# A hybrid recurrent block on one core: RWKV-7 chunk maps combined ahead of the chain, buffers and PSUM banks reallotted

## The chip, the cores and the metric

One Trainium2 chip, one core. The metric is the device time of one execution in microseconds (us), the median of several runs.

## What is computed

Two layers over 1024 tokens of width 1024, batch 1, all in float32. Layer 0 mixes with a gated DeltaNet (GDN, 4 heads of 128) and an RWKV-7 group (8 heads of 64); layer 1 mixes with an RG-LRU. Each mixer and each SwiGLU FFN (width 2816) has adaptive norms around it. What the change touches is the RWKV-7 recurrence; per token and head, with a state `S` of 64 by 64:

```
def step(S, inp):
    r_t, w_t, k_t, v_t, kk_t, b_t = inp
    sa = -jnp.einsum('bhvk,bhk->bhv', S, kk_t)
    S = S * w_t[:, :, None, :] + sa[..., None] * b_t[:, :, None, :] + v_t[..., None] * k_t[:, :, None, :]
    return S, jnp.einsum('bhvk,bhk->bhv', S, r_t)
```

The kernel doesn't step by tokens but by chunks of 64: within a chunk the recurrence is a triangular system, whose inverse is made for all chunks at once, and a short chain then carries the state from chunk to chunk.

## The kernel before

The program is written with a framework that places instructions by their order in the program and by what is ready, gives each tile one of its tag's buffers, and sets all semaphores. Each engine then runs its own list in order, so an instruction that waits holds up what is behind it. A full-precision product is made of three float32r products (high by high, high by low, low by high); small products are plain float32, which the trace shows as two records each.

The two halves of the sequence (512 tokens, `h`) go through the mixer in 16 groups: for each half, four GDN heads and four pairs of RWKV heads, alternating. `mixer` (L947) runs three tasks per step beside each other: `inputs` of group n (projections in `mm` banks, 24 wide matmuls each), the first part of group n-1 (`gdn_first` L1219 or `rwkv_first` L1401, both around `inverse` L1164), and the second part of group n-2 (`gdn_second` L1288 or `rwkv_second` L1471, the chain). `together` (L151) hands out turns so that the tasks advance by their expected number of steps (`COUNTS`, L31). So a step with an RWKV chain has a GDN inverse beside it, and a step with an RWKV inverse has a GDN chain.

`rwkv_first` works on a pair of heads (head 0 on partitions 0 to 63, head 1 on 64 to 127) and all 8 chunks at once. `each` (L1410) issues sixteen 64 by 64 products into one bank of tag `sa` (three banks); `masked` and `turned` make masked score matrices and transposed operands. Its results are Z (the inverse), abq, btk, u, yv and kv. `rwkv_second` then does, for each chunk, three visits to TensorE with VectorE between them (banks of tag `sb`, two of them):

```
self.mm(pc[j, 0:64], ar[j, c, 0], S[j])
nc.vector.tensor_tensor(rhs, pc[:, 0:64], u[:, c], ALU.add)
self.mm(pc[j, 64:128], Z[j, c], rhs[j])
nc.vector.tensor_scalar(sa, pc[:, 64:128], -1.0, 0.0, ALU.mult, ALU.add)
self.mm(po[j, 0:64], btk[j, c], sa[j])
stt(S, po[:, 0:64], egc[:, c:c + 1], se, ALU.mult, ALU.add)
```

with two more products into `po` for the chunk's output, and norms and gate at the end of the eight chunks.

Other places that the change touches: `ffn.operands` (L696) makes the FFN's operand sums out of the second half of the tokens, with the transposes in `mm` banks (two of them) and all four work tiles of a round in tag `ad` (four buffers); `first` (L680) runs beside it and uses `mm` banks and two `e` buffers. `lru` (L808) makes, per block, two branch projections, four gate products and two z projections; all projections are in `mm` banks. `down` (L576) holds back the last `ntail` slices of its second half, so that each token tile finishes while matmuls of the next still run; at two places the held weights lie in tag `cy`.

Of the kernel before, what the change touches and what calls it, by code (L numbers as in the profile page):

```python
# [32 lines left out]
M_BANKS = ("mm", "mm", "es", "sa", "mm", "mm", "es", "sa")  # L33
G_TAGS = ("p",) * 6 + ("s1",) * 4 + ("cy",) * 6 + ("ar",) * 2 + ("s2",) * 2 + ("e",) * 2
RSCALE = 1024.0
# [37 lines left out]
class Block:  # L73
# [77 lines left out]
    def together(self, tasks):  # L151
# [12 lines left out]
        return out  # L164

    def gemm_fm(self, ps, w, xs):
        self.now(self.gemm_steps(ps, w, xs))
# [51 lines left out]
    def pair(self, tag):  # L219
        if tag == "ar":  # L220
# [420 lines left out]
    def ffn(self, l, hs):  # L641
# [54 lines left out]
        def operands(xs):  # L696

            tags = iter(("p",) * 12 + ("s1",) * 8 + ("cy",) * 12 + ("s2",) * 4)
            A = lambda: self.t("ad", [128, 512])
            for k in range(4):  # L700
                v12 = self.modulated(self.turned_x(xs, k), *self.AB, k, "ad")
                v22 = self.modulated(self.turned_x(xs, k + 4), *self.AB, k + 4, "ad")
                (h1, l1), (h2, l2) = b11[k], b21[k]
# [6 lines left out]
                for full, out in ((d2, t2), (d1, t1), (v12, t3), (v22, b22), (None, t4)):  # L710
                    if full is None:
                        tt(d2, f32(h2), d2, ALU.subtract)
                        tt(d2, d2, f32(l2), ALU.add)
                        full = d2
                    if out is t4 and k > 1:
                        hi, lo = self.pair("ar")
                    else:
                        hi, lo = self.t(next(tags), [128, 512], F32R), self.t(next(tags), [128, 512], F32R)
# [89 lines left out]
    def lru(self, h, hs):  # L808
# [16 lines left out]
        def branch(b):  # L825
            out = []
            for m in (2 * b, 2 * b + 1):
                ps = self.now(self.proj(w, 1024 + 128 * m, hs))
                cv = self.with_tail(ps, m, h)
                y = self.conv(ps, cv, lambda j: col["lru_conv_w"][:, 8 * j + m:8 * j + m + 1], col["lru_conv_b"][:, m:m + 1], "cy")  # L830
                out.append((y, self.split(y, "s1")))
            return out
# [3 lines left out]
        for b in range(4):  # L836
# [41 lines left out]
    def layers(self, hs, AB, x1, x2, x3, late):  # L878
# [4 lines left out]
        for n, (l, x_in, x_out) in enumerate(subs):  # L883
# [20 lines left out]
            for h in range(2):  # L904
# [24 lines left out]
                def aside():  # L929
# [3 lines left out]
                    elif n + 1 < len(subs):  # L933
# [13 lines left out]
    def mixer(self, x, x_out, mT, hs, AB):  # L947
# [7 lines left out]
        for W in (self.gW, self.rW):  # L955
            nc.gpsimd.memset(W, 0.0)
        self.pool_lo = 2
        groups = [(h, i) for h in range(2) for i in (0, 4, 1, 5, 2, 6, 3, 7)]
# [56 lines left out]
    def mix_out(self, h, x, x_out, mT, Gb, banks):  # L1015
# [12 lines left out]
        if h == 0:  # L1028
            self.down(lhs, self.a["mix_w_out"][0], h, x, x_out, Gb, banks)
        else:  # L1030
            return self.down(lhs, self.a["mix_w_out"][0], h, x, x_out, Gb, banks, "s2", ("cy", 6), True)

# [30 lines left out]

    def proj(self, w, c0, hs):
        ps = self.t("mm", [128, 512])
        yield from self.gemm_steps(ps, self.load_w(w, c0), hs)
        self.tick()
        return ps
# [274 lines left out]
    def rwkv_inputs(self, w, hs, sgd, wdad, p, h):  # L1343
# [26 lines left out]
        stt(rn, k, cl(self.col["rwkv_k_k"]), rn, ALU.mult, ALU.mult)  # L1370
        ar = self.t("ar", [128, 8, 2, 64])
        tt(ar[:, :, 0, :], c8(rn), eg[:, :, 0:64], ALU.mult)
        kf = E()
# [8 lines left out]
        r = self.shifted((yield from self.proj(w, 2056 + 128 * p, hs)), 12 + p, p, h, "e")  # L1382
        tt(ar[:, :, 1, :], c8(r), eg[:, :, 1:65], ALU.mult)
        stt(r, r, cl(self.col["rwkv_r_k"]), k, ALU.mult, ALU.mult)
# [16 lines left out]
    def rwkv_first(self, q):  # L1401
# [13 lines left out]
        def masked(x, tags):  # L1415
            lo, hi = self.t(tags[0], S8), self.t(tags[1], S8)
            for c0 in (0, 4):
                ps = bank()
                for c in range(4):
                    for j in hh:  # L1420
                        self.mm(ps[j, c * 128:c * 128 + 128], x[j, (c0 + c) * 64:(c0 + c) * 64 + 64], ar[j, c0 + c])
                yield
# [6 lines left out]
        def turned(x, tag):  # L1429
            ps = bank()  # L1430
            for i in range(4):
                self.tr(ps[:, i * 128:i * 128 + 128], x[:, i * 128:i * 128 + 128])
            yield
# [6 lines left out]

        ab, abq = yield from masked(bt, ("s1", "cy"))

# [4 lines left out]

        Z = yield from self.inverse(self.rlev, self.rtri, ab, bc(self.i64h), bc(self.i64), bc(self.i64s), prod, S8, self.rW, True)

        vtk = yield from turned(v, "s1")  # L1450
        ktk = yield from turned(kt, "s1")
        ak, akq = yield from masked(kt, ("s1", "s1"))
        pu = bank()
        each(pu, lambda j, c: ak[j, c], lambda j, c: vtk[j, c])
# [12 lines left out]
        nc.vector.tensor_tensor(kv, c8(pk), egc.unsqueeze(2).to_broadcast(S8), ALU.mult)  # L1467
        btk = yield from turned(bt, "cy")
        return Z, abq, btk, u, yv, kv

    def rwkv_second(self, q, carry, sgd, p, h):  # L1471
        nc = self.nc
        ar, bt, kt, v, bo, egc = q
        Z, abq, btk, u, yv, kv = carry
        stt = nc.vector.scalar_tensor_tensor
        hh = [slice(0, 64), slice(64, 128)]
        yT = self.t("s2", [128, 512])
        key = 4 + p
        if h == 0:
            S = self.t(f"S{key}", [128, 64])  # L1480
            nc.vector.memset(S, 0.0)
            self.S[key] = S
        for c in range(8):
            S = self.S[key]
            cs = slice(c * 64, c * 64 + 64)
            pc = self.t("sb", [128, 512])
            for j in hh:
                self.mm(pc[j, 0:64], ar[j, c, 0], S[j])
            yield
            se = self.t("ch", [128, 64])  # L1490
            stt(se, S, egc[:, c:c + 1], kv[:, c], ALU.mult, ALU.add)
            rhs = self.t("ch", [128, 64])
            nc.vector.tensor_tensor(rhs, pc[:, 0:64], u[:, c], ALU.add)
            for j in hh:
                self.mm(pc[j, 64:128], Z[j, c], rhs[j])
            yield
            sa = self.t("ch", [128, 64])
            nc.vector.tensor_scalar(sa, pc[:, 64:128], -1.0, 0.0, ALU.mult, ALU.add)
            po = self.t("sb", [128, 512])
            for j in hh:  # L1500
                self.mm(po[j, 0:64], btk[j, c], sa[j])
            for j in hh:
                self.mm(po[j, 64:128], S[j], ar[j, c, 1], stop=False)
            for j in hh:
                self.mm(po[j, 64:128], sa[j], abq[j, c], start=False)
            stt(S, po[:, 0:64], egc[:, c:c + 1], se, ALU.mult, ALU.add)
            self.act(yT[:, cs], po[:, 64:128], AF.Copy)
            yield
        nc.vector.tensor_tensor(yT, yT, yv.rearrange("p c n -> p (c n)"), ALU.add)
        pm = self.t("sb", [128, 512])  # L1510
# [41 lines left out]
```

## Time and profile before

| | us |
|---|---|
| median of 3 runs | 2840.73 |
| lowest, highest | 2827.24, 2842.32 |
| the profiled execution, its own time | 2827.93 |
| its span, first to last instruction | 2826.1 |
| TensorE busy | 2653.2 (94%) |
| VectorE busy | 1847.6 (65%) |
| ScalarE busy | 1258.8 (45%) |
| POOL busy | 659.3 (23%) |

Of the span, the mixer takes about the first 1000 us, the FFN of layer 0 and its sums run to about 1740, the RG-LRU stage to 2100, the second FFN to the end. In the profile PE is TensorE's matmuls, PEld its weight loads, DVE VectorE, ACT ScalarE, SP the queue that issues DMAs. Tile names have buffer numbers left out. The mean granted clock of TensorE was 0.977.

### The profile page before, as it was taken

Reading aid. Unit: us, or ns where it says so; the run is one execution under the profiler, and the core shown is the slowest. Engines: PE = TensorE matmul, PEld = TensorE weight load, DVE = VectorE, ACT = ScalarE, POOL = GpSimd, SP = SyncE. Lnnn points to the kernel's source line nnn. Section 1 sums busy time; section 2 is a strip of 40 time slices with the busy share of each in tenths; the row PEclk is TensorE's granted clock in tenths of the full one; section 3 lists DMA queues with packets and bytes.
Section 4 is the critical chain, followed back from the end, with each engine's and each line's share of the span. In section 5 each row is a group of like instructions: output and inputs, shape, how many; then the busy total and the mean of one; then the engine's idle time right before and its main releaser. Section 6 shows DMA issues by size and latency. Waiting matters only on the chain. (4 is left out here: it accounts for less than half of the span.)

```text
span 2826.1 us, 43754 instructions
## 1 busy us (share of the span) xinstructions
PE 2653.2 (94%) x16104; PEld 2049.9 (73%) x16104; DVE 1847.6 (65%) x3280; ACT 1258.8 (45%) x2300; POOL 659.3 (23%) x516
## 2 busy tenths in 40 slices
PE   6999999998999998899999999989898899999998
PEld 3666666666766766687888878777776788888887
DVE  5867778677687654998454463997874885444233
ACT  4555565553555535233332233664754333333222
POOL 2322221232322115333330000211214333331000
PEclk9999999999999999999999999999999999999999
DMA  7411222224521254666448873635334454448653
GB/s 234 120 44 56 61 79 61 68 57 135 161 57 53 69 186 138 225 214 209 145 138 294 293 253 117 198 105 167 102 111 149 147 194 151 141 134 290 230 188 109
DMA packets 402653, 415.75 MB, mean 147 GB/s; under 512 B 26331, under 2 KB 260606, under 8 KB 402438
## 3 DMA queue, kind: packets, MB, share of 16 engines
q1 hardware_dynamic: 402438, 412.95, 45.3%
q8 instruction: 127, 2.08, 0.3%
q14 instruction: 88, 0.72, 0.1%
HBM read 333.16 MB, written 79.69 MB: 146 GB/s over the span
## 5 line engine op out<-in xcount | busy, mean ns | idle before, releaser
L98 PE MATMUL mm<-ht,wh 128*128 128x512 f32 x2176 | 744.1, 417 | 52.7 <-ACT e L686 26.2
L98 PEld LDWEIGHTS mm<-ht,wh 128*128 128x128 f32 x2176 | 405.2, 194 | 156.0 <-ACT e L686 37.4
L98 PE MATMUL mm<-ht,wl 128*128 128x512 f32 x1088 | 446.6, 412 | 4.6 <-DVE wl L139 3.5
L139 POOL TENSOR_TENSOR wl<-wf,wh 128x512 fp32r<-128x512 f32 x144 | 207.9, 1446 | 552.6 <-ACT wh L138 417.3
L138 ACT CAST wh<-wd 128x512 fp32r<-128x512 f32 x206 | 127.3, 621 | 292.9 <-PE sb L98 219.4
L98 PEld LDWEIGHTS mm<-ht,wl 128*128 128x128 f32 x1088 | 210.8, 194 | 52.9 <-DVE wl L139 4.2
L660 POOL TENSOR_TENSOR wl<-wd,wh 128x512 fp32r<-128x512 f32 x99 | 132.6, 1339 | 487.4 <-ACT wh L659 447.8
L138 ACT CAST wh<-wf 128x512 fp32r<-128x512 f32 x215 | 133.3, 621 | 253.5 <-PE sb L98 83.2
L139 DVE TENSOR_TENSOR wl<-wd,wh 128x512 fp32r<-128x512 f32 x182 | 127.1, 700 | 167.8 <-ACT wh L138 167.7
L537 POOL TENSOR_TENSOR sm<-sm,dv 128x1 f32<-128x1 f32 x64 | 38.6, 611 | 510.9 <-DVE sm L535 277.0
L660 DVE TENSOR_TENSOR wl<-e,wh 128x512 fp32r<-128x512 f32 x88 | 62.7, 712 | 105.2 <-ACT wh L659 105.2
L98 PE MATMUL sa<-s,wh 128*128 128x512 f32 x392 | 122.9, 395 | 0.0
L659 ACT CAST wh<-wd 128x512 fp32r<-128x512 f32 x99 | 61.5, 622 | 124.2 <-PE sb L98 41.4
L106 ACT ACT_TABLE_LOAD x88 | 112.9, 1283 | 2.3 <-PEq L1541 0.7
L98 PEld LDWEIGHTS <-h 64*64 64x64 f16 (+1 forms) x1984 | 53.8, 106 | 80.5 <-issue 52.8
L659 ACT CAST wh<-yx 128x512 fp32r<-128x512 f32 x88 | 54.7, 622 | 126.8 <-PE sb L98 48.5
L106 ACT ACTIVATE e<-e 128x512 f32<-128x512 f32 x140 | 88.5, 632 | 47.4 <-DVE e L759 23.6
L106 ACT ACTIVATE e<-mm 128x512 f32<-128x512 f32 x120 | 71.4, 595 | 73.2 <-PE mm L98 70.5
L139 POOL TENSOR_TENSOR wl<-wd,wh 128x512 fp32r<-128x512 f32 x24 | 34.8, 1450 | 271.0 <-ACT wh L138 231.0
L139 DVE TENSOR_TENSOR wl<-wf,wh 128x512 fp32r<-128x512 f32 x71 | 48.9, 689 | 71.7 <-ACT wh L138 69.2
L98 PE MATMUL sa<-wh,p 128*128 128x512 f32 x260 | 91.5, 397 | 0.0
L767 ACT CAST yx<-yx 128x512 fp32r<-128x512 f32 x88 | 54.8, 623 | 77.4 <-DVE yx L764 42.1
(484 smaller groups left out, 6526.5 us busy)
## 6 DMA issues: line engine op xcount, KB each, us to landing
gd<-yx SPq DMA_DIRECT2D x176, 256.0 KB, 2.2
wd<-in_ffn_w_down_dram SPq DMA_DIRECT2D x132, 256.0 KB, 3.9
wf<-in_mix_w_in_dram SPq DMA_DIRECT2D x120, 256.0 KB, 2.8
wd<-in_ffn_w_gate_dram SPq DMA_DIRECT2D x114, 256.0 KB, 2.9
wd<-in_ffn_w_up_dram SPq DMA_DIRECT2D x78, 256.0 KB, 3.1
yx<-x SPq DMA_DIRECT2D x72, 256.0 KB, 4.2
ad<-in_ada_w_dram SPq DMA_DIRECT2D x63, 256.0 KB, 3.0
wf<-in_ffn_w_gate_dram SPq DMA_DIRECT2D x62, 256.0 KB, 3.1
```

Of the source, the lines that this page charges most:

```text
L98: self.nc.tensor.matmul(out, lhsT=lhsT, rhs=rhs, start=start, stop=stop, skip_group_check=more)
L106: return self.nc.scalar.activation(out, in_, func, bias=bias, scale=scale)
L138: nc.scalar.copy(wh, wf)
L139: (nc.gpsimd if self.pool_lo and (self.pool_lo > 1 or k0) else nc.vector).tensor_tensor(wl, wf, wh, ALU.subtract)
L537: nc.gpsimd.tensor_tensor(r, r, self.mhalf[:, 0:1], ALU.pow)
L659: nc.scalar.copy(flat(wh), full)
L660: (eng or nc.vector).tensor_tensor(flat(wl), full, flat(wh), ALU.subtract)
L767: nc.scalar.copy(hi, g)
```

## The change

For each chunk the state goes through one linear map. `rwkv_first` now builds, for all eight chunks: G = -(Z applied to the transposed a), P = identity + (G by btk) as a block-diagonal 128 by 128 matrix for the pair of heads, R = (G by abq) + r, nu = -(Z applied to u), and folds nu into yv and kv. A chain step is then one matmul of P with the state and one VectorE operation; the eight states are kept, and the outputs are sixteen products with R at the end. To make this, a fourth transposed operand is needed, and the two streams in `rwkv_first` (inverse, and the rest) advance beside each other. Tag PB is new (two buffers of twice the size, in which the two P lie during the mixer); s1 has six buffers in place of eight, cy ten in place of twelve, and later users of the tags follow.

```diff
-            self.tags(self.pool("work"), p=12, ar=2, s1=8, cy=12, s2=4, st=2, gb=2, ad=4)
+            self.tags(self.pool("work"), p=12, ar=2, PB=2, s1=6, cy=10, s2=4, st=2, gb=2, ad=4)
...
-            A = lambda: self.t("ad", [128, 512])
+            A = E
             for k in range(4):
-                v12 = self.modulated(self.turned_x(xs, k), *self.AB, k, "ad")
-                v22 = self.modulated(self.turned_x(xs, k + 4), *self.AB, k + 4, "ad")
+                v12 = self.modulated(self.turned_x(xs, k, ("sb", "es")), *self.AB, k, "ad")
+                v22 = self.modulated(self.turned_x(xs, k + 4, ("sa",)), *self.AB, k + 4, "ad")
...
-                ps = self.now(self.proj(w, 128 * m, hs))
+                ps = self.now(self.proj(w, 128 * m, hs, "sb"))
...
-                               "s2" if keep else "yx", ("cy", 6) if keep else ("ht", 7) if last else (None, 0), keep, aside)
+                               "s2" if keep else "yx", ("cy", 5) if keep else ("ht", 7) if last else (None, 0), keep, aside)
...
-        ar = self.t("ar", [128, 8, 2, 64])
+        ar = self.t("ar", [128, 2, 8, 64])
...
+        (Z, abq), (atk, vtk, akq, u, btk, ktk) = yield from self.beside(inverted(), others())
+        pg = bank()
+        each(pg, lambda j, c: Z[j, c], lambda j, c: atk[j, c])
         yield
-        u = self.t("cy", S8)
-        nc.scalar.copy(u, c8(pu))
+        G = self.t("yx", S8)
+        self.act(G, c8(pg), AF.Copy, scale=-1.0)
+        ph = bank()
+        each(ph, lambda j, c: Z[j, c], lambda j, c: u[j, c])
+        pr = bank()
+        each(pr, lambda j, c: G[j, c], lambda j, c: abq[j, c])
+        yield
+        nu = self.t("cy", S8)
+        self.act(nu, c8(ph), AF.Copy, scale=-1.0)
+        R = self.t("cy", S8)
+        nc.vector.tensor_tensor(R, c8(pr), ar[:, 1], ALU.add)
+        pp = bank()
+        each(pp, lambda j, c: G[j, c], lambda j, c: btk[j, c])
+        yield
+        P = self.rP[self.turn % 2]
+        self.turn += 1
+        for j in (0, 1):
+            nc.vector.tensor_tensor(P[hh[j], :, 64 * j:64 * j + 64], c8(pp)[hh[j]],
+                                    self.i64[hh[j]].unsqueeze(1).to_broadcast([64, 8, 64]), ALU.add)
+
+        def two(ps, f, g, f2, g2):
+            for c in range(8):
+                for j in hh:
+                    o = ps[j, c * 64:c * 64 + 64]
+                    self.mm(o, f[j, c], g[j, c], stop=False)
+                    self.mm(o, f2[j, c], g2[j, c], start=False)
+
         py = bank()
-        each(py, lambda j, c: vtk[j, c], lambda j, c: akq[j, c])
+        two(py, vtk, akq, nu, abq)
...
         pk = bank()
-        each(pk, lambda j, c: ktk[j, c], lambda j, c: vtk[j, c])
+        two(pk, ktk, vtk, btk, nu)
...
+        S = self.t("s2", [128, 8, 64])
+        nc.scalar.copy(S[:, 0], self.S[key])
+        pc = self.t("sb", [128, 512])
         for c in range(8):
-            S = self.S[key]
-            cs = slice(c * 64, c * 64 + 64)
-            pc = self.t("sb", [128, 512])
+            o = pc[:, c * 64:c * 64 + 64]
+            self.mm(o, P[:, c], S[:, c])
+            yield
+            stt(S[:, c + 1] if c < 7 else self.S[key], o, egc[:, c:c + 1], kv[:, c], ALU.mult, ALU.add)
+        po = self.t("sb", [128, 512])
+        for c in range(8):
             for j in hh:
...
+                self.mm(po[j, c * 64:c * 64 + 64], S[j, c], R[j, c])
+        yield
```

`beside` takes a step of each of two generators in turn. The moved instructions show in TensorE's list at two places.

The chain, in a step with a GDN inverse and RWKV projections beside it (`mm` is a projection, `sa` the inverse, `sb` the chain; moving operand first, weights second). Before:

```order
L98 MATMUL mm_2156<-ht_367,wh_2165 128x512
L98 MATMUL mm_2156<-ht_366,wl_2166 128x512
L98 MATMUL sb_2182<-ch_2197,cy_1699 64x64 x2
L98 MATMUL mm_2156<-ht_372,wh_2165 128x512
L98 MATMUL mm_2156<-ht_373,wh_2165 128x512
L98 MATMUL sb_2216<-ch_2214,cy_1885 64x64 x2
L98 MATMUL sb_2216<-ar_1074,S_370_1938 64x64 x2
L98 MATMUL sb_2216<-cy_1185,ch_2214 64x64 x2
L98 MATMUL mm_2156<-ht_372,wl_2166 128x512
```

and now (PB is P, s is the row of states, cy is R):

```order
L98 MATMUL sa_2153<-h_403_2125,W_432 128x64
L98 MATMUL sb_2202<-cy_1869,s_381_2061 64x64 x3
L98 MATMUL mm_2253<-ht_291,wh_2256 128x512
L98 MATMUL mm_2253<-ht_292,wh_2256 128x512
L98 MATMUL sb_2063<-s_381_2061,PB_436 128x64
L98 MATMUL sb_2202<-cy_1869,s_381_2061 64x64
L98 LDWEIGHTS h_402_2123
L98 MATMUL sa_2169<-h_404_2127,h_402_2123 128x64
```

The visits of two and of six narrow products are gone; a 128 by 64 product stands for them, and the output products are strewn between other work.

The end of the first part, in a step with a GDN chain beside it (`sa` with 64x64 is the RWKV pair of heads). Before:

```order
L98 MATMUL mm_2993<-ht_384,wh_3002 128x512
L98 MATMUL sa_3103<-s_577_3044,s_580_3065 64x64 x8
L98 MATMUL mm_2993<-ht_385,wh_3002 128x512
L98 MATMUL mm_2993<-ht_384,wl_3003 128x512
L98 MATMUL sa_3127<-s_581_3066,s_577_3044 64x64 x16
L98 MATMUL mm_3161<-ht_291,wh_3164 128x512
L98 MATMUL mm_3161<-ht_292,wh_3164 128x512
L98 MATMUL mm_3161<-ht_291,wl_3165 128x512
L98 MATMUL sa_3179<-s_577_3044,s_579_3060 64x64 x16
L98 MATMUL mm_3161<-ht_297,wh_3164 128x512
```

and now:

```order
L98 MATMUL sa_1822<-cy_1411,cy_1786 64x64 x15
L98 MATMUL sa_1839<-cy_1189,yx_1820 64x64 x16
L98 MATMUL sb_1858<-cy_1002,ch_1856 128x128
L98 MATMUL mm_1751<-ht_372,wh_1760 128x512
L98 MATMUL mm_1751<-ht_373,wh_1760 128x512
L98 MATMUL mm_1751<-ht_372,wl_1761 128x512
L98 MATMUL sa_1871<-cy_1458,yx_1820 64x64 x16
L98 MATMUL mm_1751<-ht_378,wh_1760 128x512
L98 MATMUL mm_1751<-ht_379,wh_1760 128x512
L98 MATMUL mm_1751<-ht_378,wl_1761 128x512
L98 MATMUL sa_1893<-s_278_1280,yx_1274 64x64
L98 MATMUL sa_1893<-cy_1189,cy_1867 64x64
```

Where blocks of sixteen stood, there are more of them, and the last two blocks alternate between two products that are summed in one place.

## Rows read from the trace of the kernel before

**Rows 1.** the page, busy time by engine, share of the span, instructions
```profile
PE 2653.2 (94%) x16104; PEld 2049.9 (73%) x16104; DVE 1847.6 (65%) x3280; ACT 1258.8 (45%) x2300; POOL 659.3 (23%) x516
```

**Rows 2.** the chain that ended last, one piece: start, us, engine, tile, line, matmuls
```profile
2216.60 2.72 PE sa L98 x12
```

**Rows 3.** windows, RWKV-chain step, GDN-chain step: busy PE, PEld, DVE, ACT, POOL; clock, DMA
```profile
192.00:248.00 56.00, 52.03 (x425) 35.36 (x424) 42.05 (x92) 29.94 (x59) 15.18 (x11) 0.97 0.16 43
248.00:292.00 44.00, 43.46 (x571) 32.01 (x570) 34.43 (x68) 28.41 (x53) 11.52 (x9) 1.00 0.27 80
```

**Rows 4.** TensorE in order of time in an RWKV-chain step: start, us, tiles, records
```profile
974.49 0.39 PE L98 MATMUL mm<-ht,wl 128*128 128x512 f32 x1
974.81 0.33 PE L98 MATMUL sb<-ch,cy 64*64 64x64 f32 x4
974.98 0.28 PE L98 MATMUL sb<-ar,S 64*64 64x64 f32 x4
975.09 0.28 PE L98 MATMUL sb<-cy,ch 64*64 64x64 f32 x4
975.30 0.73 PE L98 MATMUL mm<-ht,wh 128*128 128x512 f32 x2
975.88 0.39 PE L98 MATMUL mm<-ht,wl 128*128 128x512 f32 x1
...
976.46 0.73 PE L98 MATMUL mm<-ht,wh 128*128 128x512 f32 x2
977.12 0.33 PE L98 MATMUL sb<-ch,cy 64*64 64x64 f32 x4
977.38 0.50 PE L98 MATMUL mm<-ht,wl 128*128 128x512 f32 x1
```

**Rows 5.** the same in a GDN-chain step: narrow blocks, transposes, GDN chain
```profile
964.96 3.06 PE L98 MATMUL sa<-s,s 64*64 64x64 f32 x96 [0.44 <-ACT s L1438]
967.96 0.66 PE L101 MATMUL sa<-k,p 128*128 128x128 f32 x4
968.45 0.39 PE L98 MATMUL sb<-ch,cy 128*128 128x128 f32 x2
968.67 0.39 PE L98 MATMUL sb<-cy,S 128*128 128x128 f32 x2
968.89 0.39 PE L98 MATMUL sb<-cy,ch 128*128 128x128 f32 x2
969.04 0.48 PE L98 MATMUL mm<-ht,wh 128*128 128x512 f32 x1
```

**Rows 6.** tile ch on VectorE: duration ns min/median/max, first and last start
```profile
L1491 DVE SCALAR_TENSOR_TENSOR ch<-S,egc,cy x64: 269/279/1309, 187.9 to 996.5; 128x64 f32<-128x64 f32 x64
L1493 DVE TENSOR_TENSOR ch<-sb,cy x64: 209/218/226, 195.7 to 997.3; 128x64 f32<-128x64 f32 x64
L1498 DVE TENSOR_SCALAR ch<-sb x64: 206/225/227, 197.8 to 999.3; 128x64 f32<-128x64 f32 x64
```

**Rows 7.** waits of TensorE in the mixer, 110 to 1003 us: total, times, longest
```profile
PE sa L98 <- DVE h L1192: 10.9, 9, 1.6
PE sb L98 <- DVE ch L1493: 7.0, 7, 1.6
```

**Rows 8.** RG-LRU stage: a wait of TensorE, and windows of both halves
```profile
PE mm L98 <- DVE cy L857: 9.6, 3, 5.5
...
1760.00:1910.00 150.00, 137.73 (x605) 111.67 (x604) 138.55 (x265) 99.91 (x164) 28.38 (x24) 0.97 0.46 147
1940.00:2090.00 150.00, 136.15 (x572) 109.00 (x572) 135.15 (x219) 94.14 (x155) 27.27 (x23) 0.94 0.44 140
```

**Rows 9.** FFN operands: waits of TensorE in both layers, window of the first
```profile
PE mm L98 <- ACT e L686: 9.4, 5, 4.6
...
PE mm L98 <- ACT e L686: 8.7, 4, 4.6
...
1100.00:1150.00 50.00, 34.68 (x126) 26.23 (x125) 39.24 (x44) 23.15 (x41) 26.02 (x17) 0.83 0.38 121
```

More of the change, by code (lines that the diff above doesn't have):

```diff
@@ L33 @@
 M_BANKS = ("mm", "mm", "es", "sa", "mm", "mm", "es", "sa")
[L34 removed]
+G_TAGS = ("p",) * 6 + ("s1",) * 3 + ("cy",) * 5 + ("PB",) * 2 + ("ar",) * 2 + ("s2",) * 2 + ("e",) * 2
 RSCALE = 1024.0
@@ L164, in together, with beside @@
         return out
+    def beside(self, a, b):
+        left, out = {0: a, 1: b}, {}
+        while left:
+            for j, steps in list(left.items()):
+                try:
+                    next(steps)
+                except StopIteration as e:
+                    out[j] = e.value
+                    del left[j]
+            yield
+        return out[0], out[1]
     def gemm_fm(self, ps, w, xs):
@@ L219, in pair @@
     def pair(self, tag):
-        if tag == "ar":
+        if tag in ("ar", "PB"):
             u = self.t(tag, [128, 2, 512], F32R)
@@ L714, in operands @@
                         full = d2
-                    if out is t4 and k > 1:
-                        hi, lo = self.pair("ar")
+                    if out is t4:
+                        hi, lo = self.pair("ar" if k > 1 else "PB")
                     else:
@@ L830, in branch @@
                 y = self.conv(ps, cv, lambda j: col["lru_conv_w"][:, 8 * j + m:8 * j + m + 1], col["lru_conv_b"][:, m:m + 1], "cy")
-                out.append((y, self.split(y, "s1")))
+                out.append((y, self.split(y, "PB" if m % 2 else "s1")))
             return out
@@ L956, in mixer @@
             nc.gpsimd.memset(W, 0.0)
+        self.turn = 0
+        self.rP = [self.t("PB", [128, 8, 128]) for _ in range(2)]
+        for P in self.rP:
+            nc.gpsimd.memset(P, 0.0)
         self.pool_lo = 2
@@ L1030, in mix_out @@
         else:
-            return self.down(lhs, self.a["mix_w_out"][0], h, x, x_out, Gb, banks, "s2", ("cy", 6), True)
+            return self.down(lhs, self.a["mix_w_out"][0], h, x, x_out, Gb, banks, "s2", ("cy", 5), True)
     def mixer_params(self, w):
@@ L1062, in with_tail, with proj @@
         return cv
-    def proj(self, w, c0, hs):
-        ps = self.t("mm", [128, 512])
+    def proj(self, w, c0, hs, bank="mm"):
+        ps = self.t(bank, [128, 512])
         yield from self.gemm_steps(ps, self.load_w(w, c0), hs)
@@ L1431, in turned @@
             for i in range(4):
-                self.tr(ps[:, i * 128:i * 128 + 128], x[:, i * 128:i * 128 + 128])
+                self.tr(ps[:, i * 128:i * 128 + 128], x(i))
             yield
@@ L1439, in turned @@
             return y
-        ab, abq = yield from masked(bt, ("s1", "cy"))
+        pair = lambda x: lambda i: x[:, i * 128:i * 128 + 128]
         def prod(ps, x, y):
@@ L1446, in prod, with inverted @@
                     self.mm(ps[j, c], x[j, c], y[j, c])
[L1448 to L1454, printed above, removed]
-        yield
-        u = self.t("cy", S8)
-        nc.scalar.copy(u, c8(pu))
+        def inverted():
+            ab, abq = yield from masked(bt, ("s1", "cy"))
+            Z = yield from self.inverse(self.rlev, self.rtri, ab, bc(self.i64h), bc(self.i64), bc(self.i64s), prod, S8, self.rW, True)
+            return Z, abq
@@ new lines, in others @@
+        def others():
+            atk = yield from turned(pair(ar[:, 0].rearrange("p c n -> p (c n)")), "yx")
+            vtk = yield from turned(pair(v), "yx")
+            ak, akq = yield from masked(kt, ("s1", "s1"))
+            pu = bank()
+            each(pu, lambda j, c: ak[j, c], lambda j, c: vtk[j, c])
+            yield
+            u = self.t("cy", S8)
+            nc.scalar.copy(u, c8(pu))
+            btk = yield from turned(pair(bt), "cy")
+            ktk = yield from turned(pair(kt), "yx")
+            return atk, vtk, akq, u, btk, ktk
@@ L1467, in rwkv_first @@
         nc.vector.tensor_tensor(kv, c8(pk), egc.unsqueeze(2).to_broadcast(S8), ALU.mult)
-        btk = yield from turned(bt, "cy")
-        return Z, abq, btk, u, yv, kv
+        return P, R, yv, kv
     def rwkv_second(self, q, carry, sgd, p, h):
@@ L1473, in rwkv_second @@
         ar, bt, kt, v, bo, egc = q
-        Z, abq, btk, u, yv, kv = carry
+        P, R, yv, kv = carry
         stt = nc.vector.scalar_tensor_tensor
         hh = [slice(0, 64), slice(64, 128)]
-        yT = self.t("s2", [128, 512])
         key = 4 + p
         if h == 0:
-            S = self.t(f"S{key}", [128, 64])
-            nc.vector.memset(S, 0.0)
-            self.S[key] = S
-        for c in range(8):
-            S = self.S[key]
-            cs = slice(c * 64, c * 64 + 64)
-            pc = self.t("sb", [128, 512])
-            for j in hh:
[L1488 to L1508, printed above, removed]
@@ L1509, in rwkv_second @@
-        nc.vector.tensor_tensor(yT, yT, yv.rearrange("p c n -> p (c n)"), ALU.add)
+            self.S[key] = self.t(f"S{key}", [128, 64])
+            nc.vector.memset(self.S[key], 0.0)
+        S = self.t("s2", [128, 8, 64])
+        nc.scalar.copy(S[:, 0], self.S[key])
+        pc = self.t("sb", [128, 512])
+        for c in range(8):
+            o = pc[:, c * 64:c * 64 + 64]
+            self.mm(o, P[:, c], S[:, c])
+            yield
+            stt(S[:, c + 1] if c < 7 else self.S[key], o, egc[:, c:c + 1], kv[:, c], ALU.mult, ALU.add)
@@ L1510, in rwkv_second @@
+        po = self.t("sb", [128, 512])
+        for c in range(8):
+            for j in hh:
+                self.mm(po[j, c * 64:c * 64 + 64], S[j, c], R[j, c])
+        yield
+        yT = self.t("s2", [128, 512])
+        nc.vector.tensor_tensor(yT, po, yv.rearrange("p c n -> p (c n)"), ALU.add)
         pm = self.t("sb", [128, 512])
```

8 lines of the change are left out of this document (4 added, 4 removed).

## The prediction

> **What bounds the kernel now.** I read the page first, then busy time in windows, then the waits, then the instructions of TensorE in order of time. The page gives TensorE 94% of the span [rows 1]. That figure is flattering, since ends of matmuls are modelled and a matmul whose successor stands waiting still counts. A better measure is the spacing of starts: in the chain that ended last, twelve matmuls of 512 columns take 2.72 us, 0.227 us each [rows 2], and wherever starts follow at that step TensorE is the bound.
>
> The windows show that the mixer alternates between two kinds of steps [rows 3]. In the first kind (call it A) the program puts the RWKV chain of one head pair beside the GDN inverse of the next heads and the RWKV projections of the ones after. In the second kind (B) it puts the GDN chain beside the RWKV inverse and the GDN projections. A takes 56 us, with 425 matmul records, B takes 44 us with 571. There are eight of each. A has fewer matmuls and is longer: its TensorE stands in small waits and in changes between wide and narrow matmuls. B is packed; what is added there is paid in full. This decides the case, because the change takes matmuls out of A and puts more into B.
>
> **What leaves A.** A chunk of the chain had three visits of 64-row matmuls on TensorE. The visit with twelve records stands between wide matmuls: from 974.49 to 975.88 us there are three wide ones (0.68) in 1.39 us, so the visit costs 0.71 [rows 4]. The visit of four records: from 976.46 to 977.38 us there are two wide ones (0.45) in 0.92, so 0.47 [rows 4]. Twelve records back to back would be about 0.39 (0.17, 0.11, 0.11 between their starts), so some 0.3 us of a visit is going in and out. A chunk is 0.71 + 2 x 0.47 = 1.65 us; times 8 chunks and 8 head pairs, 106 us. To this come TensorE's waits for the sum before the second visit, 7 us [rows 7]. Together 113 us.
>
> **What takes its place in A.** One matmul per chunk, 128 rows by 128 columns, with 64 moving columns: two records. The trace has no such shape; the nearest is the GDN chain's two records of 128 by 128, which start 0.22 us apart from the next pair and pass into wide matmuls with no 0.3 us in between [rows 5]. I take 0.25 us: 64 x 0.25 = 16 us (0.22 to 0.52 each: 14 to 33). The sixteen output matmuls of a head pair stay narrow, and the order above shows them strewn in ones, twos and threes, about ten visits. Ten visits with half of them beside other narrow matmuls cost about 8 x 0.3 + 16 x 0.06 = 3.2 us, 26 us in all; in one block they would cost 1.3 (10 us), each alone 5.8 (46 us). So 42 us stand where 113 stood: **minus 71 us** (minus 34 to minus 89).
>
> **What B gets.** Ninety-six narrow records (three blocks of sixteen matmuls) take 3.00 us back to back, 1.0 us a block [rows 5]; in and out adds the 0.3 of above. Four new blocks (the products G, h, R and P): 5.2 us. The two blocks that become sums of two products double: each gets sixteen more matmuls, and now two matmuls of the same head follow each other. Four records of two heads take 0.17 us, which are three slots of 0.055 [rows 4]: only the records at a change of head overlap. A chunk of four matmuls then has six slots, 0.34 us, and the block 2.7 in place of 1.0: 3.4 us for both. Four more transposes take 0.5 [rows 5]. That is 9.1 us a head pair, and over eight **plus 73 us** (52 if all runs dense and overlapped, 88 if the sums don't overlap at all).
>
> So TensorE's own account of the mixer is even: plus 2 us, between minus 37 and plus 54. What tips it is small. VectorE loses three of four chain operations, 0.28, 0.22 and 0.22 us [rows 6], 46 us in all, and gets about 2 us a head pair for R and P. A has VectorE at 42 of 56 us [rows 3], and the waits of TensorE for it that are not the chain's are led by the inverse's masked copies, 10.9 us [rows 7]. I take minus 8 (0 to minus 15). A's granted clock is 0.97 and B's 1.00 [rows 3]; of the 1.7 us that this costs each A, I take back 5 us in all (0 to 10). ScalarE swaps eight small copies for four transposed copies, two full ones and a small one; it is busy 30 of 56 us [rows 3], and costs nothing unless it falls behind in B. The two memsets on POOL lie before the first chain, where POOL is a quarter busy; zero. The mixer: **minus 11 us**.
>
> **Outside the mixer.** In the RG-LRU stage the z projections move from the two mm banks to the two sb banks. TensorE waited 9.6 us for VectorE to give back an mm bank there [rows 8]; its order doesn't change. But VectorE is busy 139 and 135 of 150 us in the two halves [rows 8], so a wait that goes leaves at most 11 and 15 us until VectorE itself is the pace, and I take minus 8 (0 to minus 15). When the FFN operands are made, TensorE waited 9.4 and 8.7 us for ScalarE's copy out of an mm bank, which stood behind casts, which stood behind the four ad buffers [rows 9]. The change gives the transposes other banks and the differences the eight e buffers, two rounds ahead in place of one. VectorE has 39 of 50 us there [rows 9]; I take minus 7 and minus 6 (together plus 4 to minus 25). What is late next is VectorE in both. The held tail of two down projections loses one of six slices, 12 wide matmuls of cover or 2.7 us [rows 2] in each; it covers work that is short, so plus 2 (0 to 5). Loads of gated values only change tiles: zero, DMA is a matter of the same bytes.
>
> **Sum.** Minus 11, 8 and 13, plus 2: minus 30 us. The profiled execution took 2827.9 us (2826.1 of span); the median of the three runs is 2840.7, 12.8 above. So 2798 by the one and **2811 us** by the other, which is what I forecast, 1.1% faster. A measurement here can tell about 0.5%, 14 us: faster means under 2826.5, slower over 2855.
>
> **Rivals.** *Slower: three sa banks for two streams.* In B the inverse holds two sa banks at a time, and now seven other products and transposes run beside it on the same three. TensorE takes instructions in order, so a bank not yet copied out stops the projections too. Such waits exist: nine on the inverse, 1.2 us each [rows 7]. One for each of seven new users in eight head pairs is 67 us: 2878 us. It decides from three such waits a head pair on, since 3 x 8 x 1.2 eats the 30 us. Against it: ScalarE and VectorE have a third of B free [rows 3]. Chance 0.13. *A doesn't shrink.* TensorE is relieved there, but the weights, the inverse's chain and VectorE keep A near its length, and only 25 us of the 71 come back: 2811 + 46 = 2857. For it: A's other waits; against: VectorE has a quarter of A free. Chance 0.07. *No change.* The mixer is even and the waits outside only move to VectorE, minus 5 in all instead of minus 21, and the mixer's small gains fail: 2838. Chance 0.17. *B hides the added work.* Weight loading is busy 32 of B's 44 us [rows 3]; if the 12 us left were room, the 73 us would cost nothing: 2738. Starts at the full step speak against it; chance 0.05. The Trainium skill (Perfetto Trace Analysis, Identifying the Most-Contended Engine) would judge TensorE's headroom this way, by the busy share of weight loads and not of matmuls.
>
> My forecast has the remaining 0.58. Its own spread is about 20 us either way, so some 0.07 of it lies above 2826.5. Faster: 0.51 + 0.05 + 0.05 of the third rival = 0.61. Same: 0.07 + 0.12 + 0.02 = 0.21. Slower: the rest of the first two, 0.18. The range is 2765 to 2855: below lie the last rival and a little more, above the first and half of the second.
>
> **What would show it.** Right: A near 47 us and B near 53; new narrow blocks of 32 records near 1.0 to 1.3 us and of 64 near 2.7; chain matmuls 0.22 to 0.3 before the next start; no wait of TensorE for the z operation in the RG-LRU stage and VectorE near full there. Wrong: A still over 52 us, or B over 58 with waits on sa banks, or blocks of 64 records near 2 or near 4 us.

## The result: 1.2% slower, and the profile after

The changed kernel takes 2866.82 us (median; 2862.11 to 2875.37), the kernel before, measured beside it, 2838.07. The ratio is 1.0116, 95% interval 1.0092 to 1.0141. The forecast was 2811 us, the range 2765 to 2855: the time moved the other way, and out of the range. The profiled execution of the changed kernel took 2868.7 us (span 2866.9); before it was 2827.9, which is 10 us under that kernel's median, so the two profiles lie 41 us apart and the medians 29.

Where the 41 us between the two profiled executions lie, by the last finishing sum of a half's residual (L604 before, L617 now), the first gate sum of an FFN (L744, L757) and the RG-LRU's first and last product (L874, L887), each by its start:

| stretch | before | after | difference |
|---|---|---|---|
| start to the end of the mixer's output map | 1064.1 | 1110.3 | +46.2 |
| from there to the FFN's first gate sum (operands, layer 0) | 84.6 | 77.1 | -7.5 |
| from there to the first RG-LRU product | 658.1 | 663.4 | +5.3 |
| first to last RG-LRU product | 271.5 | 266.7 | -4.8 |
| from there to the last finishing sum | 53.9 | 56.8 | +2.9 |
| operands, layer 1 | 81.9 | 81.0 | -0.9 |
| the rest | 612.0 | 611.6 | -0.4 |

One profile of each kernel gives the mixer's loss only roughly. Two of the experiments below leave the mixer as it was: up to 1000 us, TensorE's list in e4 is that of the kernel before, and in e3 that of the changed kernel. Their output maps end at 1075.8 and 1101.0 us, so the loss is some 25 to 46 us. The 5.3 us in the third row are not the change's: in e8 and e13, which have the old code there, this stretch takes 663.7 and 664.0 us.

The page's first part, answering to [rows 1]: 672 matmul records more, and VectorE's total a little down.

```profile
PE 2673.6 (93%) x16776; PEld 2102.3 (73%) x16776; DVE 1838.6 (64%) x3112; ACT 1252.4 (44%) x2283; POOL 663.1 (23%) x518
```

The loss is in the mixer. Windows of the changed kernel, an A step, a B step and the next A (columns as in [rows 3]):

```profile
203.00:252.00 49.00, 44.09 (x225) 30.45 (x223) 31.28 (x57) 23.46 (x40) 11.93 (x9) 0.81 0.17 44
252.00:312.00 60.00, 57.92 (x858) 46.59 (x856) 42.21 (x82) 32.45 (x67) 11.78 (x9) 0.98 0.21 59
312.00:360.00 48.00, 42.57 (x227) 29.39 (x227) 33.54 (x57) 25.09 (x44) 13.12 (x10) 0.86 0.24 66
```

A is about as long as forecast (47), but with 225 records. By the prediction's own account it should have had 425 - 160 + 48 = 313; some 90 records of it now run in B, which is 60 us and not 53. So where A and B meet has moved, and the pair tells more: 109 us where 100 stood before, and where 100 were forecast. A has half the records of before and seven eighths of the time. And its granted clock has fallen from 0.97 to 0.81 and 0.86.

What happens in A is plain in TensorE's list where the chain begins (start, us, tiles, records; in brackets the idle time before, and who ended it):

```profile
324.27 0.62 PE L98 MATMUL mm<-ht,wh 128*128 128x512 f32 x2
324.73 0.39 PE L98 MATMUL mm<-ht,wl 128*128 128x512 f32 x1
327.60 0.43 PE L98 MATMUL sb<-s,PB 128*128 128x64 f32 x2 [2.49 <-ACT s L1537]
327.85 0.48 PE L98 MATMUL mm<-ht,wh 128*128 128x512 f32 x1
...
330.14 0.69 PE L98 MATMUL sb<-cy,s 64*64 64x64 f32 x6
330.76 1.22 PE L98 MATMUL mm<-ht,wh 128*128 128x512 f32 x2
331.77 0.52 PE L98 MATMUL sb<-s,PB 128*128 128x64 f32 x2
332.23 0.47 PE L98 MATMUL sb<-cy,s 64*64 64x64 f32 x2
332.63 0.40 PE L98 MATMUL sa<-h,h 128*128 128x64 f16 x4
332.96 0.47 PE L98 MATMUL sb<-cy,s 64*64 64x64 f32 x2
333.36 0.79 PE L98 MATMUL mm<-ht,wl 128*128 128x512 f32 x1
```

The first chain product waits 2.49 us. What follows is narrow, with few wide matmuls between, and from 329.3 us the granted clock is at 1.2 GHz for 13.7 us: two wide matmuls from 330.76 to 331.77 take 0.5 us each, where 0.23 is the full step. In the 15 us between the first chain product and the last there are 14 wide matmuls, 3.2 us of work at that step. In all eight chains together there are 117 wide matmuls in 104 us, some 15 a chain.

But the clock fell in five of the eight only: these take 13 to 18 us, at a granted clock of 0.52 to 0.65, and before four of them TensorE waits 2.2 to 2.5 us. The other three (at 553.5, 837.1 and 1026.7 us) wait 0.1 to 1.0 us, stay at 1.00 and take 8 to 10 us. Nor does the order alone settle it. The fifth chain has the same list and the same wait of 2.50 us in the changed kernel and in e3; here is the stretch behind that wait in the one and in the other:

```profile
674.00:690.00 16.00, 16.00 (x92) 11.87 (x92) 5.97 (x18) 3.66 (x8) 1.27 (x1) 0.50 0.10 34
...
669.00:680.00 11.00, 10.74 (x95) 7.98 (x95) 6.36 (x19) 4.31 (x11) 1.29 (x1) 1.00 0.14 51
```

Why the first chain product waits: ScalarE's copy of the carried state (L1537) stands in ScalarE's list behind an activation that waits for VectorE's scan of the projections (L1377):

```profile
323.04 0.69 ACT L106 ACTIVATE e<-es,dv 128x512 f32<-128x512 f32 x1 [0.47 <-PE es L98]
326.72 0.63 ACT L106 ACTIVATE e<-e 128x512 f32<-128x512 f32 x1 [3.00 <-DVE e L1377]
327.31 0.24 ACT L1537 COPY s<-S 128x64 f32<-128x64 f32 x1
```

TensorE's waits from 110 to 1000 us, longest first (engine, tile, line, waited for: total us, times, longest). Those on the chain's VectorE sum [rows 7] are gone; the copy leads in their place:

```profile
PE sb L98 <- ACT s L1537: 11.2, 6, 2.5
PE sa L98 <- DVE h L1216: 8.5, 7, 2.6
```

What the lower level costs can be read where TensorE, after a long idle time, runs wide matmuls alone (changed kernel, end of the mixer): starts 0.43 us apart, then 0.24.

```profile
1048.61 0.80 PE L98 MATMUL mm<-wh,p 128*128 128x512 f32 x1 [5.53 <-DVE p L110]
...
1051.69 0.63 PE L98 MATMUL es<-wh,p 128*128 128x512 f32 x1
1052.11 0.63 PE L98 MATMUL es<-wl,p 128*128 128x512 f32 x1
1052.54 0.60 PE L98 MATMUL es<-wh,p 128*128 128x512 f32 x1
1052.97 0.41 PE L98 MATMUL sb<-wh,p 128*128 128x512 f32 x1
1053.21 0.40 PE L98 MATMUL sb<-wl,p 128*128 128x512 f32 x1
```

From 110 to 1050 us the clock was at 1.2 GHz for 41 us before and for 97 us after; at nearly half speed the 56 us more are worth up to 28. In the second profile of each mixer (e4, e3) it was 55 and 92 us, so a difference of some 15 us between two kernels in this figure can be chance.

The diff does not show what set this order: `COUNTS` (L31) is not in it. `together` gives the next turn to the task with the smallest share of its expected steps done. The line says 25 steps for the chain and 28 for the RWKV first part. The changed code has 9 and 21; before it had 24 and 23. So the chain gets its nine turns in the first 36% of A, and the first part is through after three quarters of B.

### The profile page after: what moved, and what is told of

The parts are those of the page before. It is cut to its first block, busy times and chain, and to the rows that moved or that the text cites. A ratio compares the mean times of both kernels' runs of the same rounds, so it can differ in the third digit from the quotient of the medians.

```text
span 2866.9 us, 44925 instructions
## 1 busy us (share of the span) xinstructions
PE 2673.6 (93%) x16776; PEld 2102.3 (73%) x16776; DVE 1838.6 (64%) x3112; ACT 1252.4 (44%) x2283; POOL 663.1 (23%) x518
## 5 line engine op out<-in xcount | busy, mean ns | idle before, releaser
L98 PE MATMUL mm<-ht,wh 128*128 128x512 f32 x1920 | 664.7, 422 | 31.1 <-ACT e L699 20.3
L98 PEld LDWEIGHTS mm<-ht,wh 128*128 128x128 f32 x1920 | 359.5, 196 | 121.4 <-ACT e L699 32.3
L98 PE MATMUL mm<-ht,wl 128*128 128x512 f32 x960 | 394.1, 413 | 11.3 <-DVE wl L139 10.1
L98 PEld LDWEIGHTS mm<-ht,wl 128*128 128x128 f32 x960 | 187.3, 195 | 53.7 <-DVE wl L139 11.8
L98 PEld LDWEIGHTS <-h 64*64 64x64 f16 (+1 forms) x1984 | 60.4, 108 | 92.6 <-issue 51.3
L98 PE MATMUL sb<-p,wh 128*128 128x512 f32 x264 | 82.7, 395 | 5.8 <-DVE yx L759 5.8
```

The lines of the kernel that those rows point to most:

```text
L98: self.nc.tensor.matmul(out, lhsT=lhsT, rhs=rhs, start=start, stop=stop, skip_group_check=more)
```

## The experiments

The theories. **T1**: the chain's order in A (stall, few wide matmuls around narrow ones, lower clock) is the loss. **T2**: the added narrow work in B is the loss, and A is bound by other things. **T3**: the edits outside the mixer. Medians are set beside the kernel before as run in the same batch.

**e1_direct_state.** The copy stays, but the first chain product no longer needs it:

```diff
-            self.mm(o, P[:, c], S[:, c])
+            self.mm(o, P[:, c], S[:, c] if c else self.S[key])
```

> The first chain matmul of a head pair reads the carried state itself; ScalarE's copy of it stays, but only the output products need it. In the changed kernel TensorE stands 2.5 us there in five of the first six RWKV-chain steps looked at or less, and works at half the granted clock right behind. Theory 1 (the stall and the clock that falls behind it are the loss): the waits for that copy go, 8 x 2.5 = 20 us at least, and the time at half clock (211 us) falls by 30 to 50 us, worth half of that: 2825 to 2850 us. Theory 2 (the added narrow work in the other steps is the loss, and the chain's steps are bound by the inverse and VectorE): the idle moves to the next wait, 2860 to 2870. Theory 3 (the edits outside the mixer): no change, 2867.

2841.14 us, ratio to before 1.0024 (0.9996 to 1.0051): 26 us under the changed kernel. It is not the wait itself that came back: listed waits of TensorE between 110 and 1000 us sum to 65 us, against 67. The first wait of the chain shrank, others (L1209, 10.3 us) grew:

```profile
PE sb L98 <- ACT s L1537: 3.4, 3, 1.5
```

But the first chain product now stands earlier in the list (201.7 us, in place of 218.5), some 37 wide matmuls lie between the first product and the last in place of 15 (most of them before the second; the other seven products keep 9 to 15 among them), and the time at 1.2 GHz over the whole run falls from 210 to 152 us. Of these 58 us, 55 lie before the end of the mixer's output map, which comes 26 us earlier. 58 us of it gave 26, 0.45 each, with waits and output visits (65, against 71) nearly unchanged. The Trainium skill (TensorE: Matmul & The Clock Gate, HAM oscillation — how this bites in real kernels) counts half of the time at the lower clock as lost; that would be 29 us here, as an estimate, and this run agrees within what it can tell.

**e2_counts.** The one line the change had left alone:

```diff
-COUNTS = ((33, 24, 13), (25, 28, 25))
+COUNTS = ((33, 24, 13), (25, 21, 10))
```

> COUNTS says how many steps a task is expected to have; the changed chain has 9 where 25 stands and the changed first part 21 where 28 stands, so the chain runs through in the first 40% of its step. Here 10 and 21. Theory 1: the chain's narrow matmuls are spread among wide ones over the whole step, the half-clock time falls from 211 us towards 160, and the chain's norm goes later: 2840 to 2855 us. Theory 2: the length of the steps is set by the inverse and by the added blocks, 2860 to 2872. It could also be slower, if the chain's end now falls into the next, packed step: up to 2885.

2793.18 us, ratio 0.9843 (0.9817 to 0.9869): 74 us under the changed kernel, far beyond the expectation, and 1.6% faster than before. Windows of A, B and the next A:

```profile
203.00:240.00 37.00, 35.91 (x262) 26.35 (x262) 31.08 (x65) 22.74 (x40) 11.22 (x8) 1.00 0.19 51
240.00:301.00 61.00, 59.49 (x834) 44.93 (x832) 40.07 (x76) 36.09 (x72) 13.79 (x10) 1.00 0.28 75
301.00:340.00 39.00, 34.40 (x245) 25.10 (x245) 33.01 (x66) 20.52 (x35) 10.83 (x8) 0.96 0.20 55
```

B is as long as in the changed kernel; A falls from 48 to 38 us, at nearly full clock. A chain takes 16 to 22 us (the last, which stands alone, left out), not less than before the line was mended (8 to 18), but now with 50 wide matmuls within it. Its list:

```profile
209.18 0.39 PE L98 MATMUL mm<-ht,wl 128*128 128x512 f32 x1
209.40 0.33 PE L98 MATMUL sb<-s,PB 128*128 128x64 f32 x2
209.54 0.71 PE L98 MATMUL mm<-ht,wh 128*128 128x512 f32 x2
210.09 0.40 PE L98 MATMUL mm<-ht,wl 128*128 128x512 f32 x1
...
224.65 1.15 PE L98 MATMUL sb<-cy,s 64*64 64x64 f32 x32
225.73 0.50 PE L98 MATMUL mm<-ht,wh 128*128 128x512 f32 x1
```

A chain product costs 0.14 us between wide ones, and the sixteen output products stand in one visit of 1.08. This decides against T2 as the cause: the narrow work in B is the same here.

**e5_counts_direct** puts both together.

> The corrected COUNTS and the direct state together. With the counts alone TensorE still waits once, 2.8 us, for the copy of the state, and is at half clock 27 us in the mixer. Theory 1a (the stall on the copy is a loss of its own): 3 to 8 us under 2793. Theory 1b (the rushed chain was the cause, and the stall one of its effects): the same 2793, plus or minus 4.

2796.29 us, ratio 0.9864 (0.9845 to 0.9883), not distinguishable from e2. Theory 1b: with a fitting order the stall on the copy all but vanishes by itself (2.8 us, once, in e2), and nothing is left to repair.

**e6_second_only and e10_first_only** mend one count each.

```diff
-COUNTS = ((33, 24, 13), (25, 28, 25))
+COUNTS = ((33, 24, 13), (25, 28, 10))
...
+COUNTS = ((33, 24, 13), (25, 21, 25))
```

> Only the chain's count is mended (10 for 25), the first part's stays at 28 where 21 are left. If the chain rushing through its step is the loss: 2793 to 2805 us. If the rushed first part, which leaves the last quarter of the other steps without its narrow blocks, has a share in it: 2810 to 2835.

> Only the first part's count is mended (21 for 28), the chain's stays at 25 where 9 are left. The fourth cell of the two counts: neither 2867, chain's alone 2822, both 2793. If the two act apart: 2793 + 45 = 2838 us. If the chain's stall comes from the first part having ended too early in the step before, this alone brings most of it: 2793 to 2805. If the rushed chain is a loss whatever stands before it, and the bigger one: 2845 to 2860.

Chain's count alone: 2821.94 us, 0.9956 (0.9941 to 0.9971). First part's alone: 2817.88 us, 0.9934 (0.9915 to 0.9954). Each brings 45 to 49 of the 74 us, so they share some 20, and they bring it in different coin:

| kernel | us | listed waits of TensorE, 110 to 1000 us | at 1.2 GHz, 110 to 1050 us | wide matmuls within a chain | output visits, all chains |
|---|---|---|---|---|---|
| before | 2838 | 49 | 41 | | |
| after | 2867 | 67 | 97 | 15 | 71 |
| e1 direct state | 2841 | 65 | 58 | 37 | 65 |
| e6 chain's count | 2822 | 66 | 27 | 35 | 22 |
| e10 first part's count | 2818 | 47 | 58 | 21 | 45 |
| e2 both counts | 2793 | 44 | 27 | 50 | 16 |
| e11 outputs together | 2872 | 88 | 102 | 15 | 8 |

(Waits are the sum of the listing; the fifth column is the typical chain.) With the chain's count (2822, in the second case of its expectation) the clock comes back and the output products gather, while the waits stay; the copy still holds up TensorE in seven of eight steps:

```profile
PE sb L98 <- ACT s L1537: 12.0, 7, 2.5
```

With the first part's count the waits go, the copy's with them (2.4 us, once), and the clock comes back in part. So the stall hangs on the first part's count, as e10's second case said, but it is not "most" of the loss: 2818 lies in none of the three cases. By which instructions an early end of the first part delays the copy was not traced.

**e11_outputs_together**, on the changed kernel:

```diff
+        S2 = self.t("e", [128, 8, 64])
+        nc.scalar.copy(S2, S)
...
-                self.mm(po[j, c * 64:c * 64 + 64], S[j, c], R[j, c])
+                self.mm(po[j, c * 64:c * 64 + 64], S2[j, c], R[j, c])
```

> The changed kernel with its own COUNTS; the sixteen output products read a copy of the eight states made when the chain is through, so that they stand in one visit of TensorE and not in nine strewn ones; one more ScalarE copy of 0.6 us a head pair. Theory 1c (the narrow visits in the chain's stretch, together with the stall, take the clock down): 55 visits fewer at 0.3 us, 16 us, and the half-clock time in the mixer from 99 us to 60 or less, another 20: 2828 to 2840. Theory 1d (the stall alone takes the clock down, and the strewn products cost little): 2855 to 2867.

2871.77 us, 1.0131 (1.0091 to 1.0172): no gain, against theory 1c. There are 8 visits where 71 were, and the chains themselves gain: first to last product they take 66 us in all where 104 stood, mostly at full clock. But the clock is at 1.2 GHz as long as before, now in stretches behind the chain (10.2 us from 240.2, for one), and waits elsewhere took what the visits gave. TensorE stood longer for the GDN inverse and the products behind it:

```profile
PE sa L98 <- ACT cy L1219: 21.1, 5, 6.4
PE sb L98 <- ACT s L1537: 11.2, 6, 2.5
```

Here the narrow matmuls taken out of A saved nothing, as there was no wide work left to put in their place.

**e7_sequence.** Inverse and other products one after the other, with counts that fit (27 steps, 28 stands; chain 10).

```diff
-        (Z, abq), (atk, vtk, akq, u, btk, ktk) = yield from self.beside(inverted(), others())
+        Z, abq = yield from inverted()
+        atk, vtk, akq, u, btk, ktk = yield from others()
```

> Inverse and the other products one after the other as before the change, with the count that this has (27, 28 stands), and the chain's count 10. The prediction's rival of three sa banks for two streams: without the streams beside each other the time falls under 2793, to 2780. If the banks hold nothing up, the stream of others that runs in the inverse's gaps is worth a little, and the time is 2793 to 2815.

2821.3 us, 0.9953 (0.9938 to 0.9968): 28 us slower than e2. Two streams on three `sa` banks hold nothing up that matters; running them beside each other is worth more than was expected. The mixer's output map ends 30 us later than in e2. TensorE's idle time up to there is 15 us longer, the time at 1.2 GHz is the same (47 us from the start); the other 15 us are busy time, in wider spacing of the records, and what spaced them was not found.

**e9_blocks_twice.** e2 with each of the four new blocks issued twice, so that half of that work is useless.

```diff
         each(pg, lambda j, c: Z[j, c], lambda j, c: atk[j, c])
+        each(pg, lambda j, c: Z[j, c], lambda j, c: atk[j, c])
...
```

> The corrected COUNTS, and each of the four new blocks of sixteen products (G, h, R, P) issued twice: 4 x 8 more blocks of 32 records. The prediction's term for such a block was 1.3 us, paid in full, since the steps of the first part are packed: 32 x 1.3 = 42 us, and with the second one right behind the first (no way in and out) 32 x 1.0 = 32: 2825 to 2835 us. If these steps had room for them (the rival that TensorE hides the added work): 2793 to 2800.

2816.16 us, 0.9932 (0.9909 to 0.9954): 23 us more for 32 blocks, 0.72 each, between the two cases of its expectation. A doubled block takes 2.02 us to the next start, so one block is 1.0; the step hides about a quarter of it.

```profile
286.21 2.08 PE L98 MATMUL sa<-yx,cy 64*64 64x64 f32 x64
288.23 0.49 PE L98 MATMUL sb<-ch,cy 128*128 128x128 f32 x2
```

**e8_before_rushed.** The kernel before with the fault put in, `COUNTS` (25, 28, 62):

> The kernel before with the fault put in: 62 stands for the chain's 24 steps, so that it runs through in the first 40% of its step, as in the changed kernel. If rushing is the mechanism whatever the chain is made of: TensorE waits for VectorE in the chain (7.0 us before), the half-clock time in the mixer (41 us) doubles, and the time is 2870 to 2920 us. If it is only that the changed chain is thin: the old chain has twelve products a chunk to fill its own waits, 2838 to 2850.

2827.24 us, 0.9968 (0.9953 to 0.9983): not slower, even a little faster, so my general form of T1 falls. The old chain takes 33 to 41 us where it took 43 to 51 (the last one, which stands alone, left out), with the clock at 1.2 GHz for 44 us in the mixer (41 before). With three visits of TensorE and three VectorE operations a chunk it did not run through in 15 us, though its turns came in the first 40% of the step. In the kernel before, this wrong count did no harm; it did once the chain was short enough to obey it.

**e13_before_counts.** The kernel before, with its own true counts, (25, 23, 24), as its first part too had a wrong one.

> The kernel before with its own true step counts, 23 for the first part (28 stands) and 24 for the chain (25 stands). In the changed kernel the mended count of the first part alone gave 49 us. If the table was as wrong for the kernel before, and what the mended table gives is no matter of this change: 2790 to 2815 us. If the old chain, which the order can't rush, doesn't mind when the first part ends: 2825 to 2842, and the gain from the mended table belongs to the change.

2842.59 us, 1.0019 (1.0006 to 1.0032): nothing gained. The mended table is worth 74 us to the short chain and nothing to the long one, so what e2 wins over the kernel before, 1.6%, belongs to the combined maps and the other edits.

**e12_first_18.** `COUNTS` (25, 18, 10), to see whether more helps.

> COUNTS with 18 for the first part, which has 21 steps, and 10 for the chain. If more of the first part at the step's end goes on paying as from 28 to 21: 2785 us or less. If it should end with its step: what is left over runs alone behind the others, 2798 to 2815.

2810.21 us, 0.9909 (0.9876 to 0.9942): 17 us worse than with the true number.

**e3_old_outside and e4_before_outside** take the edits outside the mixer out of the changed kernel, and put them alone into the kernel before (banks of the operands' transposes, `A = E`, the z projections' bank).

> The changed mixer with the old banks and work buffers where the FFN operands are made, and with the old banks of the RG-LRU's z projections. Theory 3 (operands in the changed kernel took 61 us where they had taken 53, in layer 0): 2855 to 2862 us. Theories 1 and 2 (the loss is the mixer's 35 us): the same 2867 or, if the z banks gave what the prediction said, up to 2880.

> The kernel before with only the two bank and buffer edits outside the mixer. The prediction's steps gave them minus 8 (RG-LRU) and minus 13 (operands): 2817 us. Going by the distances between marks in the trace of the changed kernel, the RG-LRU gives about 5 and the operands cost up to 8: 2835 to 2842.

e3: 2878.91 us, 1.0157 (1.0126 to 1.0187), some 12 us above the changed kernel. e4: 2829.03 us, 0.9976 (0.9958 to 0.9994), 8 us under before. Both ways the edits help; T3 falls, and so does the reading of operands that "cost 8", which came from comparing first instructions of unlike orders.

## Why the prediction was wrong

**The step that failed** is the new chain's place in A: "42 us stand where 113 stood: minus 71 us" prices it by what its instructions take on TensorE, at full clock, and sets its waits at nothing; beside it stand minus 8 us for waits and "take back 5 us" for the clock. The account of work itself came out. From the start to the end of the mixer's output map (idle is all time without a matmul record; the last row counts time at 1.2 GHz half):

| us | before | e4, the same mixer | after | e3, the same mixer | e2 |
|---|---|---|---|---|---|
| length | 1064.1 | 1075.8 | 1110.3 | 1101.0 | 1034.2 |
| TensorE idle | 85 | 87 | 106 | 105 | 79 |
| busy at 1.2 GHz | 57 | 81 | 129 | 108 | 40 |
| busy, as at full clock | 951 | 948 | 940 | 942 | 935 |

Work fell by 6 to 11 us, where plus 2 (minus 37 to plus 54) was forecast. What grew is what was set at nothing or less: idle time by 18 to 21 us, and the clock took half of 27 to 72 us more, 13 to 36. With the counts mended both fall below the kernel before, and the output map ends 30 us before the old one (42 before e4's); the forecast's sum for the mixer had been minus 11.

**The order was in view and not read to the end.** The prediction counted the output visits (about ten; 71 in eight chains) but not the wide matmuls between one chain product and the next. Fifteen wide ones are 3.4 us; the eight products, with VectorE between them, take 8 to 10 us from first to last at full clock and 13 to 18 where the clock fell. And the numbers that made this order stood in `COUNTS`, for a chain whose steps the diff cuts from 24 to 9. They were as loose for the old first part (28 for 23), which e13 shows to have cost nothing.

**Clock: "take back 5 us"** had the wrong sign: 13 to 36 us lost in the mixer. A's clock was taken to rise as narrow matmuls became fewer. What the rows show before it fell, four times out of five, is a wait of 2.2 to 2.5 us and then narrow work with some 15 wide matmuls in it; after the same wait and 35 wide ones it mostly stayed up (e6), and without the wait it fell less (e1), though seven of a chain's eight products still had only 9 to 15. Which of the two does it by itself is not shown, and e3's fifth chain had both and kept the clock.

**Sizes.** In an order that fits, a chain product takes 0.14 us (0.25 forecast) and the outputs 1.08 us a pair (3.2 forecast; 8 x 0.3 + 16 x 0.06 is 3.4). A block of 32 records takes 1.0 to 1.3, as forecast. A two-sum block of 64 records takes 2.06 us to the next start in e2, where 2.7 was forecast and "near 2" stood among its signs of being wrong: groups of four records follow at 0.115 us, where 0.17 was taken. Over sixteen blocks that is some 10 us of B's 73.

**Outside.** RG-LRU minus 4.8 in the trace (minus 8 forecast): the waits for the z operation [rows 8] are gone, but those for VectorE's low parts of the weights grew, as "VectorE is late next" says. 1790 to 2120 us:

```profile
PE mm L98 <- DVE wl L139: 10.1, 4, 5.1
PE sa L98 <- DVE wl L139: 8.2, 7, 1.9
```

Operands minus 7.5 and minus 0.9 (minus 7 and minus 6). The tail after the RG-LRU plus 2.9 (plus 2). Alone in the kernel before, the z and operands edits are worth 8 us, where 21 were forecast.

**Rivals.** Three `sa` banks: refuted by e7; B took 60 us, over the 58 named as a sign, but with only 1.2 us of waits before products into those banks in the window shown. A doesn't shrink, 2857 us: by its time it came nearest, with the chance put at 0.07, but A's window shrank to 49 us and it is the pair of steps that grew. Its reason (weights, the inverse's chain, VectorE keep A long) is half right: e11 shows TensorE standing for the inverse once the chain is out of the way, while e2 shows that A can be 37 us. B hides the added work: refuted by e9 but for a quarter. The Trainium skill (Perfetto Trace Analysis, Identifying the Most-Contended Engine) would read room in B off the weight loads' busy share, beside the share of peak arithmetic. Weight loads are busy 44.9 of 61 us in e2's B, and e9's added blocks were still paid at 0.72 us each.

Left open: the 15 us of wider spacing in e7, and why the same list behind the same wait keeps the clock in one execution and not in another. Whether more of the stall would go with the copy on another engine was not tried, since e5 left nothing to gain.

## What to carry to other kernels

When a change shortens a task that a hand-made table interleaves with others, read the table as part of the change: here one line of expected step counts was worth 74 us, more than every term of the diff. Price a shortened chain by the round it takes from engine to engine, and count the wide work that its new order leaves between the rounds; here it was less than the round, and what was taken out of the chain came back as idle time and as a lower clock. Instructions removed from the bound engine were worth their time only where something else stood ready in their place (e2 against e11).

## What was not expected

The clock cost about as much as the waits, in one pair of profiles more. In e1 the listed waits stayed (67 and 65 us), and 26 us came back with 58 us less at 1.2 GHz. Two executions of one mixer order differ by little but the clock: e4's profile ends the mixer 12 us later than that of the kernel before, with idle time within 2 us and 25 us more at 1.2 GHz. In e6 TensorE waited for the same copy seven times, 12.0 us, and the clock was at 1.2 GHz for 27 us only: about the same idle time, followed by a chain with 35 wide matmuls within it in place of 15, did not take the clock down for long.
